# Convolution units summed into one half of a PSUM bank, with the convolution reading the bank

## The chip, the cores and the metric

The kernel runs on one core of one Trainium2 chip. The metric is the device time of one execution in microseconds (us), the median of several runs.

## What is computed

A trunk of two layers over 256 tokens of width 1024, in float32. Each layer is half a gated feed-forward block, a token mixer, cross-attention into 256 memory tokens, and half a feed-forward block, all with RMS norms. Layer 0's mixer is dilated window attention beside a gated linear recurrence (RG-LRU); layer 1's is a chunked gated DeltaNet with 8 heads of 128 and chunks of 64. What matters here are the two places with a causal convolution of four taps over time, right behind an input projection:

```
xc  = causal_dwconv(xr, conv_w) + conv_b                 # layer 0, 512 channels of h @ w_in
qkv = silu(causal_dwconv((h @ w_in)[..., :3*W], conv_w)) # layer 1, 3 x 1024 channels
q, k, v = split(qkv);  q, k = l2norm(q), l2norm(k)
kkt  = einsum(k*beta, k) * decay                         # per head and chunk of 64
sol  = triangular_solve(I + strict_lower(kkt), [v*beta, k*beta*exp(gcum)])
qk   = einsum(q, k) * decay                              # then the recurrence over four chunks
```

## The kernel before, in words

**Numbers.** Weights and activations are held as two fp32r parts, high (index 0) and low (1); a product is high x high + high x low + low x high. Activations lie with channels on partitions and 256 tokens along the row. A weight block of 1024 x 256 comes by DMA as two halves of four 128-row blocks (`raw`, L135); each is split by ScalarE (high part, L148) and then VectorE (low part, L149) into a `wt` tile of 128 x 1024 for each part. Four `wt` tiles exist, so two units' worth.

**Units.** A unit is 256 output columns of a projection, worked as two halves of 128 columns (j = 0, 1), each 8 k-steps. In `unit` each half takes a PSUM bank of its own, seen as 128 x 2 x 256: per k-step L190 multiplies the high weights with both parts of the activations (512 columns, both regions) and L194 the low weights with the high part (256 columns, region 0). When a half is summed up, `take` is called. `add` (L260, L261) brings the two regions together in SBUF: ScalarE copies region 1 to a tile `xn` (two buffers), VectorE adds region 0. `conv` then reads `xn`: ScalarE makes the last tap (L1022 in layer 1, with its own line in layer 0), VectorE adds the three others (L1025: rows of 255, 254 and 253 columns). Layer 0 has two such units (`lru_in`), layer 1 twelve: k, q and v, four each. z units (`unit_t`, L206 and L210, whose stationary side is the activations) have no convolution and use `add`. `parts` (L232) is the form used in cross-attention: three 256-column matmuls per k-step, all into one region. In the mixers the banks come from one pool of three (`psw`); two other pools of banks (`pss`, `psf`) hold small products.

**Layer 1 around the units.** After the softplus chain (small VectorE steps) the cumulative decay goes through a transpose (L1007) and `gt` (L1008) by DMA (`gd`, then four loads of `e`, L1067) to GpSimd, which adds a mask to each of four `e` tiles (L1071); ScalarE makes exps of them (L1076). GpSimd also makes the inverse roots `rs_dn` (L331) of the heads' square sums (L1054, `ss` at L1057), which VectorE uses in `hb_all` (L1098), `nb_all` (L1097) and `rq_all` (L1145). `na` (L1119) is the k x k product (L1113) times `e`. For a group of two head pairs `na` goes by DMA (L1123, L1178) into `nb`, where VectorE inverts 16x16 blocks in 15 pairs of steps (`tm` L1183, `ti` L1185), and by DMA again (L1191, L1197) into `tu`, with which TensorE builds the inverse of the whole triangle (L1218, L1226).

**Order.** Units are written in a fixed order (k0 k1 q0 q1 k2 v0 k3 v1 z0, then v3 z1 beside the first group's recurrence, v2 q2 q3 z2, and z3 beside the second's), with a few steps put off by a count of half units. The compiler's scheduler then sets the order of each engine's instructions; an engine executes them in that order, each waiting for its own inputs and for the buffers that it writes. Two engines do not touch one bank at the same time: an instruction waits until the other engine's instructions on that bank that stand ahead of it are done.

Of the kernel before, what the change touches and what calls it, by code (L numbers as in the profile page):

```python
# [18 lines left out]
P = 128  # L19
# [47 lines left out]
class Net:  # L67
# [166 lines left out]
    def unit_split(self, name, c0, mov, dst, tokens=False):  # L234

        wts = self.w(name, c0)
        bank = self.bank_w()
        for j, ks in STEADY:
            js = slice(j * P, j * P + P)
            for k in ks:  # L240
                w, m = wts[k // 4][:, k % 4], mov[:, k]
                a, b = (m, w) if tokens else (w, m)
                self.parts(bank[:, j], [a[:, i, js] for i in range(2)], [b[:, i] for i in range(2)], k == 0, k == KD - 1)
            if j and ks.stop == KD:
                self.split(dst, bank)
            yield

    def unit_t(self, name, c0, mov, take):

# [509 lines left out]
    def mixer0(self, mid, kT_mem, mem_mov, gnext):  # L759
# [4 lines left out]
        with tc.tile_pool(name="m0", bufs=1, reuse_waits="tile") as mp:  # L764
# [10 lines left out]
            self.covered([self.mem_key(c, mem_mov, kT_mem) for c in range(2)], mp, C_MIX)  # L775

            def lru_in(c):
                yield from self.unit("ab_w_in", 1536 + c * 256, mov, lambda j, ps: conv(2 * c + j, ps), lead=c == 0)

            def conv(f, ps):  # L780
                x = mp.tile([P, S], F32, name="xn", bufs=2)
                self.add(x, ps)
                tap = lambda i: self.col(C_LCW + 4 * i + f)
                xc[f] = mp.tile([P, S], F32, name="xc", bufs=4)
                nc.scalar.activation(xc[f], x, AF.Identity, scale=tap(3), bias=self.col(C_CONVB + f))
                for i in (2, 1, 0):
                    d = 3 - i
                    nc.vector.scalar_tensor_tensor(xc[f][:, d:], x[:, :S - d], tap(i), xc[f][:, d:],
                                                   op0=OP.mult, op1=OP.add)
# [162 lines left out]
    def mixer1(self, mid, kT_mem, mem_mov, gnext):  # L952
# [4 lines left out]
        with tc.tile_pool(name="m1", bufs=1, reuse_waits="tile") as mp:  # L957
# [56 lines left out]

                return mp.tile([P, 4, P], F32, name=name, bufs=bufs)

            def conv(y, j, f, ps):

                x = mp.tile([P, S], F32, name="xn", bufs=2)
                self.add(x, ps)  # L1020
                tap = lambda i: self.dcw[:, 24 * i + f:24 * i + f + 1]
                nc.scalar.activation(y[:, j], x, AF.Copy, scale=tap(3))  # L1022
                for i in (2, 1, 0):
# [277 lines left out]
            def unit(step):  # L1301
# [4 lines left out]
                if kind == "z":  # L1306
# [4 lines left out]
                    return  # L1311
                a = "qkv".index(kind)
                y = mp.tile([P, 2, S], F32, name="y", bufs=YB)
                yield from self.unit("dn_w_in", a * 1024 + c * 256, mov,
                                     lambda j, ps: conv(y, j, a * 8 + 2 * c + j, ps))
                twice = 2 if step in TWICE else 1
                silu(y, twice)
                if kind == "k":
# [96 lines left out]
```

## Time and profile before

| | us |
|---|---|
| median of 3 runs (least, greatest) | 1266.36 (1265.66, 1267.34) |
| profiled execution | 1266.04 |
| its span; around it | 1264.3; 1.7 |
| TensorE busy | 1244.4 |
| VectorE busy | 936.0 |
| ScalarE busy | 747.1 |
| GpSimd busy | 85.7 |

The profile is of one execution. Times in its rows count from the start of the span. An idle engine matters only where it ends a wait of the engine that sets the end; so the table says little by itself, and the waits by stretch, further down, say more. [...] Layer 0's mixer with its two units stands at about 213 to 227 us, layer 1's twelve units at about 795 to 921.

### The profile page before, as it was taken

Reading aid. Unit: us, or ns where it says so; the run is one execution under the profiler, and the core shown is the slowest. Engines: PE = TensorE matmul, PEld = TensorE weight load, DVE = VectorE, ACT = ScalarE, POOL = GpSimd, SP = SyncE. Lnnn points to the kernel's source line nnn. Section 1 sums busy time; section 2 is a strip of 40 time slices with the busy share of each in tenths; the row PEclk is TensorE's granted clock in tenths of the full one; section 3 lists DMA queues with packets and bytes.
Section 4 is the critical chain, followed back from the end, with each engine's and each line's share of the span. In section 5 each row is a group of like instructions: output and inputs, shape, how many; then the busy total and the mean of one; then the engine's idle time right before and its main releaser. Section 6 shows DMA issues by size and latency. Waiting matters only on the chain.

```text
span 1264.3 us, 20349 instructions
## 1 busy us (share of the span) xinstructions
PE 1244.4 (98%) x7726; PEld 1107.4 (88%) x7726; DVE 936.0 (74%) x1591; ACT 747.1 (59%) x1270; POOL 85.7 (7%) x101
## 2 busy tenths in 40 slices
PE   7999999999999999999999999999999999999998
PEld 6888889888998888888888888888899998888887
DVE  6887967787668778766877756999767768777753
ACT  5766545875555655545656544775747555665543
POOL 1000020000101000011000001130001101000000
PEclk9999999999999999999999999999999999999999
DMA  7766585543544565556556555656433644565551
GB/s 240 224 209 197 183 257 187 178 141 124 193 135 150 184 195 186 178 185 234 177 187 192 187 188 175 164 172 173 137 97 106 200 134 153 184 197 184 176 192 65
DMA packets 228409, 221.86 MB, mean 175 GB/s; under 512 B 14920, under 2 KB 226008, under 8 KB 228184
## 3 DMA queue, kind: packets, MB, share of 16 engines
q1 hardware_dynamic: 227384, 217.42, 54.9%
q0 software_dynamic: 928, 3.15, 0.9%
q8 instruction: 60, 0.98, 0.3%
q14 instruction: 37, 0.30, 0.1%
HBM read 215.03 MB, written 5.51 MB: 174 GB/s over the span
## 4 chain that ended last, share of the span: by engine, by line
PE 76%; issue 17%; DVE 2%; DMA 2%; POOL 1%; ACT 1%; SPq 0%; POOLq 0%; DVEq 0%
PE psw L190 16%; PE pss L190 13%; PE psw L194 8%; PE psf L190 8%; PE pss L194 7%; PE psw L232 6%; PE psf L194 4%; PE psf L232 3%; PE pss L232 2%; PE psw L206 1%; PE pss L1218 1%; PE psf L1226 1%; PE psw L210 1%; DVE y L1025 1%; PE pss L1226 1%
## 5 line engine op out<-in xcount | busy, mean ns | idle before, releaser
L149 DVE TENSOR_TENSOR wt<-raw,wt 128x1024 fp32r<-128x1024 f32 (+1 forms) x406 | 484.8, 1198 | 204.9 <-ACT wt L148 202.9
L148 ACT ACTIVATE wt<-raw 128x1024 fp32r<-128x1024 f32 (+1 forms) x406 | 418.1, 1036 | 174.4 <-PE psw L194 58.0
L190 PE MATMUL psw<-x,wt 128*128 128x512 f32 x856 | 308.7, 397 | 3.2 <-DVE xn L261 3.0
L194 PE MATMUL psw<-x,wt 128*128 128x256 f32 x856 | 223.6, 282 | 0.0
L190 PE MATMUL pss<-x,wt 128*128 128x512 f32 x536 | 195.4, 396 | 1.0 <-ACT wt L148 1.0
L190 PEld LDWEIGHTS psw<-x,wt 128*128 128x128 f32 x856 | 159.2, 188 | 31.3 <-DVE xn L261 3.6
L194 PEld LDWEIGHTS psw<-x,wt 128*128 128x128 f32 x856 | 161.1, 188 | 8.8 <-issue 0.2
L194 PE MATMUL pss<-x,wt 128*128 128x256 f32 x536 | 140.3, 282 | 0.5 <-DVE wt L149 0.5
L190 PE MATMUL psf<-x,wt 128*128 128x512 f32 x344 | 124.1, 393 | 0.0
L190 PEld LDWEIGHTS pss<-x,wt 128*128 128x128 f32 x536 | 101.4, 189 | 18.8 <-ACT wt L148 1.4
L194 PEld LDWEIGHTS pss<-x,wt 128*128 128x128 f32 x536 | 101.6, 190 | 6.5 <-DVE wt L149 1.0
L194 PE MATMUL psf<-x,wt 128*128 128x256 f32 x344 | 89.5, 281 | 0.0
L326 POOL TENSOR_TENSOR acc<-acc,sq 128x256 f32<-128x256 f32 x49 | 44.5, 909 | 662.1 <-ACT sq L324 661.8
L190 PE MATMUL pss<-h,wt 128*128 128x512 f32 x242 | 87.0, 397 | 0.0
L190 PE MATMUL psw<-h,wt 128*128 128x512 f32 x242 | 86.9, 396 | 0.0
L190 PEld LDWEIGHTS psf<-x,wt 128*128 128x128 f32 x344 | 64.6, 188 | 11.0
L194 PEld LDWEIGHTS psf<-x,wt 128*128 128x128 f32 x344 | 64.8, 188 | 3.8
L194 PE MATMUL pss<-h,wt 128*128 128x256 f32 x242 | 66.0, 280 | 0.0
L194 PE MATMUL psw<-h,wt 128*128 128x256 f32 x242 | 66.0, 280 | 0.0
L190 PE MATMUL psf<-h,wt 128*128 128x512 f32 x176 | 63.3, 397 | 0.0
L190 PEld LDWEIGHTS pss<-h,wt 128*128 128x128 f32 x242 | 45.5, 188 | 9.9
L190 PEld LDWEIGHTS psw<-h,wt 128*128 128x128 f32 x242 | 45.4, 188 | 9.9
(379 smaller groups left out, 2130.2 us busy)
## 6 DMA issues: line engine op xcount, KB each, us to landing
raw<-in_ffn_w_in_dram SPq DMA_DIRECT2D x176, 512.0 KB, 3.9
raw<-in_ffn_w_out_dram SPq DMA_DIRECT2D x80, 512.0 KB, 3.5
raw<-in_xa_wkv_dram SPq DMA_DIRECT2D x32, 512.0 KB, 3.7
raw<-in_dn_w_in_dram SPq DMA_DIRECT2D x32, 512.0 KB, 4.2
raw<-in_ab_w_in_dram SPq DMA_DIRECT2D x20, 512.0 KB, 3.9
raw<-in_xa_wq_dram SPq DMA_DIRECT2D x16, 512.0 KB, 3.3
raw<-in_xa_wo_dram SPq DMA_DIRECT2D x16, 512.0 KB, 3.4
raw<-in_ffn_w_out_dram SPq DMA_DIRECT2D x16, 256.0 KB, 2.6
```

The source lines that it names most:

```text
L148: nc.scalar.activation(a, r, AF.Copy)
L149: nc.vector.tensor_sub(b, r, a.bitcast(F32))
L190: nc.tensor.matmul(out.rearrange("p a s -> p (a s)"), w[:, 0, cols], mov[:, k].rearrange("p a s -> p (a s)"), start=k == start, stop=k == ...
L194: nc.tensor.matmul(out[:, 0], w[:, 1, cols], mov[:, k, 0], start=False, stop=False)
L206: nc.tensor.matmul(out.rearrange("p a s -> p (a s)"), mov[:, k, 0, tok], w.rearrange("p a s -> p (a s)"), start=k == 0, stop=k == KD - 1)
L210: nc.tensor.matmul(out[:, 0], mov[:, k, 1, tok], w[:, 0], start=False, stop=False)
L232: self.nc.tensor.matmul(out, a[u], b[w], start=first and i == 0, stop=last and i == 2)
L326: (eng or nc.gpsimd).tensor_add(self.acc, self.acc, sq)
L1025: nc.vector.scalar_tensor_tensor(y[:, j, d:], x[:, :S - d], tap(i), y[:, j, d:], op0=OP.mult, op1=OP.add)
L1218: nc.tensor.matmul(py[:, i], na[:, i], tu[:, 0, i], start=True, stop=True)
L1226: nc.tensor.matmul(pp[:, i], l[:, i], r[:, i], start=True, stop=True)
```

## The change

`unit_sum` takes the place of `unit` for the fourteen units that end in a convolution. It works with `parts`: three 256-column matmuls per k-step, all into one 128 x 256 region. The two halves of a unit use the two regions of one bank (the first unit of layer 0, whose halves are worked in turn, takes a bank for each). `conv` takes that region instead of a summed tile: ScalarE's tap and VectorE's three taps read PSUM. `add` and `xn` are gone from these units; z units and the gates' projection keep `add`.

```diff
+    def unit_sum(self, name, c0, mov, take, lead=False):
+
+        wts = self.w(name, c0)
+        bank = self.bank_w()
+        sums = [bank[:, 0], self.bank_w()[:, 0] if lead else bank[:, 1]]
+        for j, ks in (LEAD if lead else STEADY):
+            js = slice(j * P, j * P + P)
+            for k in ks:
+                w = wts[k // 4][:, k % 4]
+                self.parts(sums[j], [w[:, i, js] for i in range(2)], [mov[:, k, i] for i in range(2)], k == 0, k == KD - 1)
+            if ks.stop == KD:
+                take(j, sums[j])
+            if len(ks) == 4 or j:
+                yield
...
-                yield from self.unit("ab_w_in", 1536 + c * 256, mov, lambda j, ps: conv(2 * c + j, ps), lead=c == 0)
+                yield from self.unit_sum("ab_w_in", 1536 + c * 256, mov, lambda j, x: conv(2 * c + j, x), lead=c == 0)
...
-            def conv(y, j, f, ps):
+            def conv(y, j, f, x):
 
-                x = mp.tile([P, S], F32, name="xn", bufs=2)
-                self.add(x, ps)
                 tap = lambda i: self.dcw[:, 24 * i + f:24 * i + f + 1]
                 nc.scalar.activation(y[:, j], x, AF.Copy, scale=tap(3))
...
-                yield from self.unit("dn_w_in", a * 1024 + c * 256, mov,
-                                     lambda j, ps: conv(y, j, a * 8 + 2 * c + j, ps))
+                yield from self.unit_sum("dn_w_in", a * 1024 + c * 256, mov,
+                                         lambda j, x: conv(y, j, a * 8 + 2 * c + j, x))
```

`conv` of layer 0 loses the same two lines. Lines of the changed kernel are 15 higher from `add` on in the front part, 13 higher between the two mixers' `conv`s and 11 higher behind the second, so L148, L149 and L232 stay, L1025 becomes L1036, L1054 L1065, L1076 L1087, L1119 L1130 and L1218 L1229. There are 672 matmuls in these units where there were 448, each with its weight load.

The order moves too. Because the second half of a unit must wait for the convolution of the first, the scheduler puts another unit's half between them: k0's first, k1's first, k0's second, k1's second, and so on through the mixer.

TensorE before, at the end of k2's second half (`psw_8353`) and the start of v0 (`psw_8388`, a bank of its own for each half):

```order
L190 MATMUL psw_8353<-x2_79,wt_8223 128x512
L194 MATMUL psw_8353<-x2_79,wt_8223 128x256 x2
L190 MATMUL psw_8353<-x2_79,wt_8223 128x512
L190 MATMUL psw_8388<-x2_79,wt_8312 128x512 [waits DVE_49]
L194 MATMUL psw_8388<-x2_79,wt_8312 128x256
L190 MATMUL psw_8388<-x2_79,wt_8312 128x512
L194 MATMUL psw_8388<-x2_79,wt_8312 128x256
```

TensorE now, inside v0's first half (`psw_8452`, weights `wt_8371` and `wt_8395`), with k2's second half (`psw_8358`) in it; L1158 is the product of q0 and k0, L1065 are square sums of a head pair:

```order
L1158 MATMUL psf_8480<-y_8139,y_7941 128x128 [waits DVE_49]
L1158 MATMUL psf_8480<-y_8139,y_7941 128x128 x3
L232 MATMUL psw_8452<-x2_79,wt_8395 128x256 [waits Activation_49]
L232 MATMUL psw_8452<-x2_79,wt_8395 128x256
L1065 MATMUL pss_8577<-ones_86,th_8398 128x1 [waits PE_49,Activation_49]
L1065 MATMUL pss_8577<-ones_86,th_8398 128x1 x3
L232 MATMUL psw_8452<-x2_79,wt_8395 128x256 [waits DVE_49]
L232 MATMUL psw_8452<-x2_79,wt_8395 128x256 x3
L232 MATMUL psw_8358<-x2_79,wt_8255 128x256 [waits DVE_49]
L232 MATMUL psw_8358<-x2_79,wt_8255 128x256 x11
L232 MATMUL psw_8358<-x2_79,wt_8274 128x256 x12
L232 MATMUL psw_8452<-x2_79,wt_8395 128x256 x6
```

v0 now starts ahead of k2's second half and is cut in two by it; its weights `wt_8395` are waited for there, on ScalarE and then on VectorE.

ScalarE before, at the exps of the fourth `e` tile (`e_7919`); `wt_8397` and `wt_8434` are the weights of k3, the unit behind v0:

```order
L1076 ACTIVATE e_7919<-e_7919,ngc_7908 128x128 [waits Pool_49]
L1031 ACTIVATE th_8295<-y_8191 128x512 [waits DVE_49,Activation_49]
L1076 ACTIVATE e_7919<-e_7919,ngc_7908 128x128 x3
L260 ACTIVATE xn_8328<-psw_8303 128x256 [waits PE_49]
L260 ACTIVATE xn_8370<-psw_8353 128x256 [waits PE_49]
L148 ACTIVATE wt_8397<-raw_8194 128x4x256 [waits DMAHW6_49]
L1022 ACTIVATE y_8298<-xn_8328,dcw_91 128x256 [waits DVE_49]
L1048 ACTIVATE th_8338<-y_8191 128x512 [waits PE_49]
L1141 ACTIVATE q1_8340<-y_8191 128x256
L1022 ACTIVATE y_8298<-xn_8370,dcw_91 128x256 [waits DVE_49]
L148 ACTIVATE wt_8434<-raw_8299 128x4x256 [waits DMAHW7_49]
```

ScalarE now, at the same exps (`e_7938`); `wt_8395` is the second half of v0's weights, `wt_8465` the first of k3's:

```order
L1087 ACTIVATE e_7940<-e_7940,ngc_7927 128x128 x3
L1042 ACTIVATE th_8350<-y_8237 128x512 [waits DVE_49,Activation_49]
L1087 ACTIVATE e_7938<-e_7938,ngc_7927 128x128 [waits Pool_49]
L1087 ACTIVATE e_7938<-e_7938,ngc_7927 128x128 x3
L1033 ACTIVATE y_8353<-psw_8358,dcw_91 128x256 [waits PE_49]
L148 ACTIVATE wt_8395<-raw_8238 128x4x256 [waits DMAHW5_49]
L1059 ACTIVATE th_8398<-y_8237 128x512 [waits DVE_49]
L1152 ACTIVATE q1_8400<-y_8237 128x256
L148 ACTIVATE wt_8465<-raw_8240 128x4x256 [waits DMAHW6_49,PE_49]
```

Behind the exps stood the weights of k3, and now there are still those of v0's second k-half, which TensorE wants ahead of k2's second half. On GpSimd the first `rs_dn` of the burst, which stood between the first and the second `e`, now stands behind the fourth.

TensorE before, at the first use of the inverse (L1218 with `tu_8381`); `psw_8941` is z1, and v3 (both halves) stands ahead of it:

```order
L206 MATMUL psw_8941<-wt_8853,x2_79 128x512 [waits DVE_49]
L210 MATMUL psw_8941<-wt_8853,x2_79 128x256
L206 MATMUL psw_8941<-wt_8853,x2_79 128x512
L210 MATMUL psw_8941<-wt_8853,x2_79 128x256
L1218 MATMUL pss_8759<-tu_8381,na_8290 128x128 [waits DMAHW1_49]
L1218 MATMUL pss_8759<-tu_8381,na_8290 128x128 x3
L206 MATMUL psw_8941<-wt_8853,x2_79 128x512
```

TensorE now, at the same place (L1229); `psw_8869` is v3's first half, `psw_9041` is z1:

```order
L232 MATMUL psw_8869<-x2_79,wt_8785 128x256 [waits DVE_49]
L232 MATMUL psw_8869<-x2_79,wt_8785 128x256 x11
L1124 MATMUL psf_8885<-y_8554 128x128 x4
L232 MATMUL psw_8869<-x2_79,wt_8800 128x256 x12
L1229 MATMUL pss_8850<-tu_8445,na_8345 128x128 [waits DMAHW1_49]
L1229 MATMUL pss_8850<-tu_8445,na_8345 128x128 x3
L206 MATMUL psw_9041<-wt_8882,x2_79 128x512 [waits DVE_49]
L210 MATMUL psw_9041<-wt_8882,x2_79 128x256
```

v3's second half and the first 12 matmuls of z1 stood ahead of the first use of the inverse and stand behind it now.

## Rows read from the trace of the kernel before

**Rows 1.** The page, busy time of the engines and their share of the span.
```profile
PE 1244.4 (98%) x7726; PEld 1107.4 (88%) x7726; DVE 936.0 (74%) x1591; ACT 747.1 (59%) x1270; POOL 85.7 (7%) x101
```

**Rows 2.** Waits of TensorE, 700 to 960 us: who for whom, total, times, longest.
```profile
PE psw L190 <- DVE xn L261: 3.0, 2, 1.5
PE pss L1294 <- DVE qk L1285: 1.6, 2, 1.3
```

**Rows 3.** Busy time by stretch: stretch, length, engines (instructions), clock, DMA share, GB/s.
```profile
213.00:229.00 16.00, 15.82 (x91) 13.65 (x90) 15.53 (x29) 10.86 (x20) 0.00 (x0) 1.00 0.55 174
815.00:830.00 15.00, 13.54 (x92) 12.14 (x90) 12.92 (x28) 9.71 (x27) 10.31 (x11) 1.00 0.55 170
842.00:861.00 19.00, 18.68 (x123) 16.72 (x122) 18.02 (x65) 14.69 (x34) 3.08 (x2) 1.00 0.50 148
```

**Rows 4.** Timeline of TensorE: start, duration, line, operation, tiles, forms, count.
```profile
201.01 4.36 PE L232 MATMUL psw<-m,wt 128*128 128x256 f32 x36
...
602.13 0.39 PE L190 MATMUL pss<-x,wt 128*128 128x512 f32 x1
...
603.18 0.39 PE L190 MATMUL pss<-x,wt 128*128 128x512 f32 x1
```

**Rows 5.** Groups of VectorE by form, 785 to 925: count, busy, mean ns, idle before.
```profile
L149 DVE TENSOR_TENSOR wt<-raw,wt 128x1024 fp32r<-128x1024 f32 x33 | 40.1, 1217 | 2.7 <-ACT wt L148 2.6
...
L1025 DVE SCALAR_TENSOR_TENSOR y<-xn,dcw,y 128x254 f32<-128x254 f32 x24 | 11.3, 476 | 0.1
L261 DVE TENSOR_TENSOR xn<-psw,xn 128x256 f32<-128x256 f32 x25 | 10.3, 416 | 0.5 <-ACT xn L260 0.4
...
L301 DVE TENSOR_TENSOR x<-xn,x 128x256 fp32r<-128x256 f32 x8 | 3.0, 417 | 0.0
```

**Rows 6.** Groups of ScalarE by form, 785 to 925.
```profile
L148 ACT ACTIVATE wt<-raw 128x1024 fp32r<-128x1024 f32 x34 | 35.8, 1059 | 7.1 <-PE psw L194 6.3 <-PE psw L210 0.8
L1022 ACT ACTIVATE y<-xn,dcw 128x256 f32<-128x256 f32 x24 | 11.9, 505 | 5.5 <-DVE xn L261 5.5
L260 ACT ACTIVATE xn<-psw 128x256 f32<-128x256 f32 x25 | 9.3, 377 | 4.8 <-PE psw L190 4.1 <-DVE y L1025 0.7
```

**Rows 7.** Timeline of VectorE at the decays, the burst and the inversion's start.
```profile
815.11 0.28 DVE L1008 COPY gt<-pss 16x128 f32<-16x128 f32 x1
...
825.10 1.26 DVE L1098 TENSOR_TENSOR hb_all<-ss,rs_dn 128x4 f32<-128x4 f32 x1 [1.01 <-POOL rs_dn L331]
826.28 1.56 DVE L1025 SCALAR_TENSOR_TENSOR y<-xn,dcw,y 128x253 f32<-128x253 f32 x1
...
834.47 0.86 DVE L1119 SCALAR_TENSOR_TENSOR na<-psf,nb_all,e 128x128 f32<-128x128 f32 x3
...
841.85 0.18 DVE L1183 TENSOR_TENSOR tm<-nb,ti 64x15 f32<-64x15 f32 x1
```

**Rows 8.** Timeline of GpSimd at the burst.
```profile
822.52 1.56 POOL L1071 TENSOR_TENSOR e<-e,dn_negup 128x512 f32<-128x512 f32 x1 [2.37 <-DMA e<-gd]
824.04 1.03 POOL L331 TENSOR_TENSOR rs_dn<-ss,mhalf 128x4 f32<-128x4 f32 x1
825.05 3.94 POOL L1071 TENSOR_TENSOR e<-e,dn_negup 128x512 f32<-128x512 f32 x3
```

**Rows 9.** Timeline of TensorE at v0's halves and the first use of the inverse.
```profile
828.24 0.50 PE L190 MATMUL psw<-x,wt 128*128 128x512 f32 x1 [1.46 <-DVE xn L261]
...
829.74 0.95 PE L1054 MATMUL pss<-ones,th 128*128 128x1 f32 x8
...
834.61 0.50 PE L190 MATMUL psw<-x,wt 128*128 128x512 f32 x1 [1.52 <-DVE xn L261]
...
869.98 1.16 PE L1218 MATMUL pss<-tu,na 128*128 128x128 f32 x8 [0.51 <-DMA tu<-d]
```

**Rows 10.** Chain of waits around the first inversion's end: start, us, what.
```profile
861.37 4.12 DMA d<-ti
...
865.55 4.38 DMA tu<-d
```

More of the change, by code (lines that the diff above doesn't have):

```diff
@@ L777, in lru_in, with conv @@
             def lru_in(c):
-                yield from self.unit("ab_w_in", 1536 + c * 256, mov, lambda j, ps: conv(2 * c + j, ps), lead=c == 0)
-            def conv(f, ps):
-                x = mp.tile([P, S], F32, name="xn", bufs=2)
-                self.add(x, ps)
+                yield from self.unit_sum("ab_w_in", 1536 + c * 256, mov, lambda j, x: conv(2 * c + j, x), lead=c == 0)
+            def conv(f, x):
                 tap = lambda i: self.col(C_LCW + 4 * i + f)
@@ L1015, in four @@
                 return mp.tile([P, 4, P], F32, name=name, bufs=bufs)
-            def conv(y, j, f, ps):
-                x = mp.tile([P, S], F32, name="xn", bufs=2)
-                self.add(x, ps)
+            def conv(y, j, f, x):
                 tap = lambda i: self.dcw[:, 24 * i + f:24 * i + f + 1]
```

## The prediction

> **What bounds the kernel now.** The page comes first: TensorE is busy 98% of the span [rows 1], so the change is worth what it does to TensorE's few waits and what it adds to TensorE's work, and freed VectorE or ScalarE time counts only where one of these engines ends a wait. The list of TensorE's waits in the second mixer then gives what there is to win: 3.0 us in two waits for the add that frees a bank, and 1.6 us in two waits for the tile `qk` [rows 2]. The busy time by stretch shows why a small change of order matters there: VectorE is busy 18.02 of 19 us while the 16x16 blocks are inverted (842 to 861), and in 815 to 830 it is busy 12.92 of 15, with GpSimd busy too. In the first mixer, where two of the units lie, TensorE is busy 15.82 of 16 us and VectorE 15.53 [rows 3]. Last, the chain of waits: the inversion's last step, two DMAs (4.12 and 4.38 us) and then L1218, which starts at 869.98 after TensorE was idle for 0.5 us [rows 9, 10]. So at 869.98 two chains meet almost exactly: TensorE's own work, and the inversion through VectorE. Whatever the change does to the order around this point decides.
>
> **Matmuls.** 224 k-steps (28 halves of 8) go from one 512-column and one 256-column matmul to three of 256 columns. Three of the old steps take 603.18 - 602.13 = 1.05 us, 0.350 each. 36 matmuls of L232 take 4.36 us: 0.121 each, or 0.117 without the last one's tail (0.28) [rows 4]. Three are 0.350 to 0.363; I take 0.354, near the lower end, as the run is longer without a wait in it than a single unit. The sum is 224 x 0.004 = 0.9 us, between 0 and 2.9. All of it lies on TensorE's path. 224 more weight loads run beside the matmuls, as in the L232 rows.
>
> **Adds.** 28 times ScalarE's copy (0.38) and VectorE's add (0.42) go [rows 5, 6]. Consecutive VectorE instructions overlap by 0.08 (825.10 + 1.26 = 826.36, the next starts at 826.28 [rows 7]), so an add is 0.34 of a full queue: 9.5 us in all, of which 16 adds, 5.4 us, lie between the projection of the gates and the end of the first inversion. The three conv steps and the first product now read the bank. An add with one operand in the bank takes 416 ns and one with both in SBUF 417 [rows 5], so I cost the other source at nothing on VectorE; on ScalarE the bank's copy is 0.13 shorter (377 against 505 [rows 6]), off the path. [...]
>
> **The bank is shared.** A unit's second half cannot start before ScalarE and three VectorE steps have read the first: unloaded 0.51 + 3 x 0.40 = 1.7 us with the ends of the waits. The new order puts another unit's half between (k0, k1, k0, k1), 8 x 0.354 = 2.8 us. That leaves 1.1 us, less than one weight split (1.14 on VectorE, 1.06 on ScalarE). It also holds all four weight buffers during a pair: the splits for the next pair can start only when a pair's second halves have used their weights.
>
> **Where it binds: the burst on GpSimd.** I walk the new order with the durations of the rows. gt, which starts the decay chain, stands behind six halves instead of seven; less about 0.6 us of waiting for VectorE's steps ahead of it I put it at 812.9 instead of 815.11. The first `e` on GpSimd starts 7.4 us after gt [rows 7, 8], at 820.3; four of them (1.5 + 3.9) and then rs_dn, which in the new order stands behind all four instead of behind the first, end at 826.8. VectorE waits for that rs_dn at hb_all, as it did at 825.10 for one `e` and one rs_dn. Behind it on VectorE are q1's conv steps, four `na` and q1's silu step, to about 830; behind those on ScalarE the last four exps, k2's conv and the split of the second half of v0's weights (order of ScalarE), to 831.8, and VectorE's half of it to 833.0. TensorE gets there earlier. In the trace it was through k2 at 828.24 - 1.6 = 826.6 [rows 9]; in the new order k2's second half (2.8) is not yet done, 12 matmuls of v0 (1.4), sums and products (1.9, two groups like 829.74's) and, as an estimate, 1.9 us of waits and longer matmuls are (0.3 to 0.5 at each of four small products that stand behind silu or softplus steps on VectorE, 0.3 of matmuls): 829.0. So it waits 2.8 us, does the sums (0.9) and the four matmuls that stand before k2's second half, and starts that at 833.8. With v0's first half done at 837.3, and 0.6 and 0.7 us of waits after it (weights of k3, conv of v0), it ends all of v0 and k3's first half at 844.3; before, with its two waits of 1.5 us, the same work ends at 834.61 + 16 steps of 0.35 + sums of 0.95 = 841.2. **TensorE is 3.1 us later.** Bounds: -2.7 if nothing waits (the two old waits gone, 0.3 of matmuls), and +6 if a split misses at each of three further pairs by 1 us.
>
> **The inversion.** Its chain is as long as before from the last `na` (834.47 + 0.86 = 835.3, with 6.5 us of DMAs to 841.85 [rows 7]). In the walk the last `na` ends at 831.5, so the inversion starts at 838.0. Between its first and last step the new order has 18 conv steps for 16, 6 splits for 4 and no add for 5: +0.8 + 2.3 - 1.7, less 0.3 of small ones, +1.1 us on 861.3 - 841.85 = 19.5. It ends at 858.6, with half a microsecond of waits 859.2: **2.1 us earlier**, so L1218's inputs come at 867.9. Bounds: 0 if the idle grows as fast as the start moves, and 5.4 if all freed VectorE time counts.
>
> **What stands ahead of L1218.** In the new order v3's second half and 12 matmuls of z1 come behind the first L1218 instead of ahead: 14 k-steps, 4.95 us (order of TensorE). TensorE's own arrival is 869.98 - 0.5 - 4.95 + 3.1 + 0.1 = 867.7; the inputs come at 867.9. What is left to do from there is 4.95 longer, plus 0.2 of slower matmuls (7 halves). So the gain or loss is 867.9 + 4.95 + 0.2 - 869.98 = +3.1 us, with mixer 0 (4 halves, 0.1; its lead unit keeps two banks, and the one shared bank has 18 other matmuls, 3.2 us, in between) +3.2. The `qk` waits behind it [rows 2] keep their matmuls around them and stay. The profiled execution is 1266.04 (span 1264.3 and 1.7 around it), the median of the runs 0.3 more: 1266.04 + 3.2 + 0.3 = **1269.5**. Note that both limits stand near +3: to win, both the inversion and TensorE must come out better.
>
> **Rivals.** *Faster: the bank wait goes and nothing takes its place.* It decides at v0's weights: if they are split before TensorE wants them, at 829, TensorE arrives 3.0 us earlier less 0.9 of matmuls, and if the inversion then ends 7 us earlier, the time is 1266.4 - 2.1 = 1264.3, or 1262.7 if the `qk` waits go with it. For it speaks that a conv step with both tensors in SBUF took 1.56 beside GpSimd's `e`, when it is 0.48 otherwise [rows 5, 7], and a step that reads the bank would not be held if the bank operand frees it. [...] Against it: adds (5.4) and one hold (1.1) sum to 6.5 of the 7 needed, and hb_all itself now waits longer. 0.18.
>
> *Same: the pairing costs what the bank waits cost.* TensorE waits about 3.0 at the burst as before, the inversion ends 4.3 us earlier, and the extra matmuls remain: 1266.4 + 0.9 = 1267.3. For it: VectorE has 5.4 us less to do. 0.30.
>
> *Slower, as walked:* 1269.5, 0.40.
>
> *Much slower: the weight bursts.* With four buffers held by a pair, each of ScalarE's 1.06 and VectorE's 1.14 stands behind whatever conv steps are queued; missing by 1 us at some 4 more of the pairs between 800 and 920, with VectorE at 18.02 of 19 us [rows 3], gives +7, 1273.5. Against it: outside the burst VectorE gets 10% lighter. 0.12.
>
> **How the numbers follow.** A measurement can tell about 0.2%, 2.5 us, from no change. Faster by more is the first rival, 0.18; within it the second, 0.30; slower by more the last two, 0.52. The forecast is the likeliest case, 1269.5. The range runs from the better part of the first rival, 1263, to the bursts, 1274, and leaves about 1 in 10 on either side; the forecast's own range is 1268 to 1271.5.
>
> **What would show it.** Right: TensorE's waits name conv steps (L1036 in the new numbering) and the split at L148 or L149 near 829 to 834, 2 to 4 us; hb_all near 826 waits over 1 us for rs_dn; L1229 starts at 867 to 869 with a wait for the DMA of tu. Wrong: no wait of TensorE over 1 us between 820 and 845, or L1229 before 865 (then faster), or waits of half a microsecond spread over every pair (then the bursts); a k-step of three matmuls above 0.36 would mis-size the first term, and conv steps above 0.5 us the second.

## The result, and the profile after

The changed kernel takes 1275.19 us (median of 6 runs, 1274.23 to 1275.87) against 1266.28 for the kernel before on the same chip: a ratio of 1.0067, interval 1.0057 to 1.0077. It is slower by 8.9 us, where the forecast was slower by 3.2 and the range ended at 1274.0. The direction was right and the size was not. The profiled execution of the changed kernel took 1275.87, its span 1274.1.

The page's first part, which answers to [rows 1]: busy time, share and instructions of each engine.

```profile
PE 1250.7 (98%) x7950; PEld 1122.7 (88%) x7950; DVE 927.1 (73%) x1563; ACT 739.2 (58%) x1242; POOL 86.9 (7%) x101
```

VectorE's busy time fell by 8.9 us and ScalarE's by 7.9, with 28 instructions less on each. TensorE's busy time rose by 6.3. So the work that was to go has gone, and it shows nowhere in the time.

**Where the time came.** The matmul on `rcol` starts a mixer and the first matmul of L190 on `m` follows it; these rows of TensorE's timeline bound layer 1's mixer (after; before they stand at 784.35 and 943.75).

```profile
22.61 0.38 PE L379 MATMUL pss<-ident,rcol 128*128 128x128 f32 x2
...
786.89 0.43 PE L379 MATMUL pss<-ident,rcol 128*128 128x128 f32 x2 [0.21 <-POOL rcol L346]
...
953.59 0.48 PE L190 MATMUL psw<-m,wt 128*128 128x512 f32 x1
```

Layer 1's mixer takes 166.70 us, 7.3 more than its 159.40 before. From the first `rcol` matmul (20.75 before) to the second are 764.28 us against 763.60: layer 0's part costs 0.7. In single profiles this varies (762.97 to 763.79 in the kernels whose layer 0 has `unit`, mm256 apart, 763.13 to 764.76 in those with `unit_sum`), and the two means are 0.7 apart too. The remaining 1.9 us of the two spans' 9.8 lie ahead of the first `rcol` matmul, in the start-up, which the change doesn't touch and which stands at 20.75 to 22.61 in the kernels of this study. Below, "the mixer's stretch" is this 159.4 or 166.7; it repeats within about half a microsecond between kernels with the same code in it, and the median of a kernel says the rest.

TensorE's waits, 700 to 970 us, after (who for whom, total, times, longest); they answer to [rows 2].

```profile
PE psf L1158 <- DVE na L1130: 2.4, 1, 2.4
PE pss L1305 <- DVE qk L1296: 2.1, 2, 1.3
PE psw L232 <- ACT wt L148: 1.5, 1, 1.5
PE pss L1229 <- DMA tu<-d: 0.6, 1, 0.6
PE psw L232 <- DVE wt L149: 0.6, 2, 0.4
PE psw L232 <- DVE ti L1196: 0.5, 1, 0.5
```

The two waits for the bank add, 3.0 us in all, are gone. In their place stand 2.4 for the chain through `na`, 1.5 for v0's weights, and 1.1 for the next weights and for the inversion's steps that the conv steps are queued among. That is +2.0; `qk` adds 0.5 and `tu` 0.1: about 2.6 us of the mixer's 7.3 are waits of TensorE.

The burst on GpSimd, after (timeline; it answers to [rows 8]), and VectorE's steps ([rows 7]).

```profile
821.66 2.23 POOL L1082 TENSOR_TENSOR e<-e,dn_negup 128x512 f32<-128x512 f32 x1 [1.38 <-DMA e<-gd]
824.56 4.50 POOL L1082 TENSOR_TENSOR e<-e,dn_negup 128x512 f32<-128x512 f32 x3 [0.67 <-DMA e<-gd]
829.03 1.03 POOL L346 TENSOR_TENSOR rs_dn<-ss,mhalf 128x4 f32<-128x4 f32 x1
```

```profile
815.27 0.27 DVE L1021 COPY gt<-pss 16x128 f32<-16x128 f32 x1
...
823.13 1.84 DVE L149 TENSOR_TENSOR wt<-raw,wt 128x1024 fp32r<-128x1024 f32 x1
...
830.10 0.16 DVE L1109 TENSOR_TENSOR hb_all<-ss,rs_dn 128x4 f32<-128x4 f32 x1 [3.33 <-POOL rs_dn L346]
...
842.41 1.23 DVE L149 TENSOR_TENSOR wt<-raw,wt 128x1024 fp32r<-128x1024 f32 x1 [2.75 <-ACT wt L148]
...
843.95 0.17 DVE L1194 TENSOR_TENSOR tm<-nb,ti 64x15 f32<-64x15 f32 x1
```

`rs_dn` now stands behind all four `e` and ends at 830.06; VectorE has waited 3.33 us for it with everything else queued behind `hb_all`. Then TensorE, after ([rows 9]):

```profile
832.59 1.16 PE L1158 MATMUL psf<-y 128*128 128x128 f32 x8 [2.38 <-DVE na L1130]
835.27 0.79 PE L232 MATMUL psw<-x,wt 128*128 128x256 f32 x2 [1.52 <-ACT wt L148]
...
874.15 1.16 PE L1229 MATMUL pss<-tu,na 128*128 128x128 f32 x8 [0.64 <-DMA tu<-d]
```

And TensorE's granted clock behind these two waits, after (stretch, length, engines, clock, DMA share, GB/s).

```profile
832.00:835.00 3.00, 1.16 (x8) 0.97 (x8) 2.71 (x10) 2.89 (x7) 0.00 (x0) 0.93 0.29 87
835.00:838.00 3.00, 2.73 (x12) 2.71 (x13) 2.62 (x6) 1.04 (x3) 0.90 (x1) 0.50 0.44 103
838.00:841.00 3.00, 3.00 (x16) 3.00 (x15) 0.40 (x3) 0.00 (x0) 1.12 (x2) 0.50 0.76 186
841.00:844.00 3.00, 3.00 (x24) 2.85 (x23) 1.59 (x3) 2.21 (x3) 0.00 (x0) 0.93 0.00 0
```

From shortly before 835 to about 841.5 TensorE runs at 0.50 of the full clock; in the profile of the kernel before, the same stretches are at 1.00:

```profile
835.00:838.00 3.00, 3.00 (x19) 2.66 (x18) 3.00 (x8) 3.00 (x6) 0.00 (x0) 1.00 0.29 89
838.00:841.00 3.00, 3.00 (x23) 2.70 (x22) 3.00 (x6) 2.23 (x4) 0.00 (x0) 1.00 0.88 198
```

In after TensorE is busy from 835.27 on and gets less done: 16 matmuls in 838 to 841, 24 in the next 3 us. What it costs is read from the chain that ended last (start, us, what):

```profile
836.06 1.60 PE pss L1065 x8
837.66 3.64 PE psw L232 x16
...
841.32 1.07 ACT wt L148
...
842.41 1.23 DVE wt L149
...
844.03 0.08 DVE tm L1194
...
849.73 1.41 PE psw L232 x12
...
853.44 0.79 PE pss L1065 x8
...
861.19 1.55 PE psw L232 x12
...
862.77 1.07 ACT wt L148
...
863.86 1.23 DVE wt L149
865.09 0.07 DVE tm L1194
...
865.67 4.30 DMA d<-ti
```

The eight products of L1065 take 1.60 there and 0.79 later in the same chain; 16 matmuls take 3.64, and at 1.41 for 12 they would take 1.88; the two ahead of them took 0.79, and the same two behind the same wait take 0.50 at the full clock (fill14, below). That is 0.81 + 1.76 + 0.29, **2.9 us**. TensorE's busy time in the mixer bears this out (stretch, length, engines, clock, DMA share, GB/s: before, after, and two kernels of the experiments that have the matmuls of after and the clock at 1.00, own_bank and nomask_after).

```profile
784.35:943.75 159.40, 154.01 (x1042) 139.09 (x1042) 133.01 (x330) 107.37 (x234) 18.44 (x18) 1.00 0.54 150
786.89:953.59 166.70, 158.65 (x1234) 151.68 (x1234) 125.04 (x306) 100.53 (x210) 19.69 (x18) 0.98 0.51 143
786.38:945.31 158.93, 154.05 (x1233) 148.18 (x1234) 122.86 (x306) 100.43 (x210) 16.95 (x18) 1.00 0.54 151
786.02:946.71 160.69, 155.72 (x1233) 148.83 (x1234) 124.40 (x306) 98.70 (x210) 11.90 (x14) 1.00 0.53 149
```

Of the 7.3 us, 2.7 are idle time of TensorE (166.70 - 158.65 against 159.40 - 154.01) and 4.6 are busy time. After's busy time is 2.9 above nomask_after's, which is what the chain gives for the half clock. The other 1.7, by which nomask_after is above own_bank, come in kernels with the two halves in one bank; no row sorts them out. The longer row of matmuls adds nothing here: own_bank is at 154.05 and the kernel before at 154.01.

The chain also shows that this time is not TensorE's alone: ScalarE's split of the next weights (841.32) waited 5.28 us until these matmuls had released the buffer, VectorE's half of the split (842.41) is queued ahead of `tm` (844.03), and `tm` is the first step of the inversion. The same happens at the inversion's end (862.77 to 865.09): the last `tm` stands behind a split that waited for 12 matmuls. So the half clock puts back both chains that meet at L1229, the inversion and TensorE's own, and neither hides the other.

### The profile page after: what moved, and what is told of

Its sections match the earlier page's. It is cut to its first block, busy times and chain, and to the rows that moved or that the text cites. A ratio compares the mean times of both kernels' runs of the same rounds, so it can differ in the third digit from the quotient of the medians.

```text
span 1274.1 us, 20744 instructions
## 1 busy us (share of the span) xinstructions
PE 1250.7 (98%) x7950; PEld 1122.7 (88%) x7950; DVE 927.1 (73%) x1563; ACT 739.2 (58%) x1242; POOL 86.9 (7%) x101
## 4 chain that ended last, share of the span: by engine, by line
PE 78%; issue 15%; DVE 2%; DMA 2%; ACT 1%; POOL 1%; SPq 0%; POOLq 0%; DVEq 0%; ACTq 0%
PE psw L190 15%; PE pss L190 13%; PE psw L232 9%; PE psf L190 8%; PE psw L194 8%; PE pss L194 7%; PE psf L194 4%; PE psf L232 3%; PE pss L232 2%; PE psw L206 2%; PE pss L1229 1%; PE psf L1237 1%; PE psw L210 1%; DVE wt L149 1%; PE pss L1237 1%
## 5 line engine op out<-in xcount | busy, mean ns | idle before, releaser
L149 DVE TENSOR_TENSOR wt<-raw,wt 128x1024 fp32r<-128x1024 f32 (+1 forms) x406 | 485.6, 1200 | 215.2 <-ACT wt L148 213.1
L148 ACT ACTIVATE wt<-raw 128x1024 fp32r<-128x1024 f32 (+1 forms) x406 | 418.0, 1036 | 186.9 <-PE psw L194 44.7
L190 PE MATMUL psw<-x,wt 128*128 128x512 f32 x624 | 226.4, 396 | 0.3 <-DVE xc L801 0.3
L190 PE MATMUL pss<-x,wt 128*128 128x512 f32 x536 | 195.8, 397 | 1.0 <-ACT wt L148 1.0
L194 PE MATMUL psw<-x,wt 128*128 128x256 f32 x624 | 162.7, 281 | 0.0
L190 PEld LDWEIGHTS psw<-x,wt 128*128 128x128 f32 x624 | 116.9, 188 | 20.9 <-issue 0.5
L190 PE MATMUL psf<-x,wt 128*128 128x512 f32 x352 | 128.0, 395 | 0.0
L232 PE MATMUL psw<-x,wt 128*128 128x256 f32 x960 | 123.6, 285 | 2.9 <-ACT wt L148 1.5
L194 PEld LDWEIGHTS psw<-x,wt 128*128 128x128 f32 x624 | 117.5, 188 | 6.7 <-issue 0.2
L232 PEld LDWEIGHTS psw<-x,wt 128*128 128x128 f32 x960 | 117.7, 191 | 4.5 <-ACT wt L148 1.7
L190 PEld LDWEIGHTS pss<-x,wt 128*128 128x128 f32 x536 | 101.6, 190 | 18.9 <-ACT wt L148 1.4
L341 POOL TENSOR_TENSOR acc<-acc,sq 128x256 f32<-128x256 f32 x49 | 44.5, 908 | 662.7 <-ACT sq L339 662.4
L190 PE MATMUL pss<-h,wt 128*128 128x512 f32 x242 | 87.0, 397 | 0.0
L190 PE MATMUL psw<-h,wt 128*128 128x512 f32 x242 | 86.9, 396 | 0.0
L190 PEld LDWEIGHTS psf<-x,wt 128*128 128x128 f32 x352 | 66.5, 189 | 11.4
L194 PEld LDWEIGHTS psf<-x,wt 128*128 128x128 f32 x352 | 66.7, 190 | 3.9
L190 PE MATMUL psf<-h,wt 128*128 128x512 f32 x176 | 63.3, 397 | 0.0
```

Source lines behind the costliest of these rows:

```text
L148: nc.scalar.activation(a, r, AF.Copy)
L149: nc.vector.tensor_sub(b, r, a.bitcast(F32))
L190: nc.tensor.matmul(out.rearrange("p a s -> p (a s)"), w[:, 0, cols], mov[:, k].rearrange("p a s -> p (a s)"), start=k == start, stop=k == ...
L194: nc.tensor.matmul(out[:, 0], w[:, 1, cols], mov[:, k, 0], start=False, stop=False)
L232: self.nc.tensor.matmul(out, a[u], b[w], start=first and i == 0, stop=last and i == 2)
L341: (eng or nc.gpsimd).tensor_add(self.acc, self.acc, sq)
```

## The experiments

The mixer's stretch is split at the first use of the inverse (L1218 before, L1229 after). All in us; the ratio is to the kernel before on the same chip.

| kernel | median | ratio, interval | stretch | to first use | behind it |
|---|---|---|---|---|---|
| before | 1266.3 to 1267.0 | 1 | 159.4 | 85.6 | 73.8 |
| after | 1275.19 | 1.0067, 1.0057 to 1.0077 | 166.7 | 87.3 | 79.4 |
| m1_only | 1274.84 | 1.0064, 1.0049 to 1.0079 | 166.7 | 87.3 | 79.4 |
| m0_only | 1268.12 | 1.0010, 1.0000 to 1.0019 | 159.3 | 85.5 | 73.8 |
| own_bank | 1267.06 | 1.0002, 0.9992 to 1.0012 | 158.9 | 84.8 | 74.2 |
| own_l1 | 1266.34 | 0.9996, 0.9987 to 1.0004 | 159.1 | 84.0 | 75.1 |
| mm256 | 1271.87 | 1.0044, 1.0029 to 1.0059 | 163.3 | 86.4 | 76.9 |
| copy | 1272.79 | 1.0044, 1.0030 to 1.0059 | 165.6 | 84.7 | 80.8 |
| own_copy | 1269.16 | 1.0019, 1.0010 to 1.0028 | 161.6 | 83.9 | 77.7 |
| fill14 | 1274.33 | 1.0061, 1.0046 to 1.0077 | 165.7 | 86.0 | 79.6 |
| nohb_after | 1271.05 | 1.0032, 1.0020 to 1.0044 | 163.4 | 84.1 | 79.4 |
| nohb_before | 1267.27 | 1.0001, 0.9991 to 1.0010 | 159.8 | 86.2 | 73.7 |
| nomask_after | 1269.19 | 1.0022, 1.0013 to 1.0032 | 160.7 | 80.0 | 80.7 |
| nomask_before | 1264.70 | 0.9984, 0.9975 to 0.9993 | 158.4 | 82.3 | 76.1 |

**One layer at a time.** m1_only and m0_only make the change in layer 1 or in layer 0 alone; the other layer's units and `conv` are as before. For m1_only, in layer 0:

```diff
-                yield from self.unit_sum("ab_w_in", 1536 + c * 256, mov, lambda j, x: conv(2 * c + j, x), lead=c == 0)
+                yield from self.unit("ab_w_in", 1536 + c * 256, mov, lambda j, ps: conv(2 * c + j, ps), lead=c == 0)
```

> The change in layer 1's mixer alone (12 units); layer 0's two units as before. Theory A (the loss is the chain gt, e, rs_dn, hb_all, conv steps, exps, weight split that holds TensorE once near 832 to 835, and a stretch at half clock behind it): nearly all of it stays, 1273 to 1275 us, with the same two waits of 2.4 and 1.5 us and 5 to 6 us at a granted clock of 0.5. Theory B (every unit pays: longer k-steps, four reads of the bank): 12/14 of the loss, 1273.9, but with waits spread over all units. The two differ in where the time goes, not in the sum.

> The change in layer 0's mixer alone (2 units). Theory A: 0.1 of matmuls and about 0.5 of a wait, 1266.5 to 1267.2. Theory B: 2/14 of 8.9, 1267.6. If it is 1268 or more, the loss is partly from the start of the kernel (a shift of the first feed-forward block), which neither theory has.

m1_only is 8.1 us slower than before and shows the same waits, and 0.51 and 0.63 of the clock in 832 to 836 and 836 to 840. m0_only is 1.3 slower by its median (its interval ends at no difference) and 0.9 by its rows up to layer 1's mixer. So the loss is layer 1's, and layer 0's term is small, though not the 0.1 of the forecast; 1268.12 is more than either theory had. A wait of 0.3 us for `xc` (TensorE, L190 <- L801) stands in both kernels that change layer 0 and not before.

**Is it the shared bank?** own_bank gives each half a bank of its own; three matmuls per k-step, no add, and the convolution reading PSUM all stay.

```diff
-        bank = self.bank_w()
-        sums = [bank[:, 0], self.bank_w()[:, 0] if lead else bank[:, 1]]
+        sums = [None, None]
...
+            if sums[j] is None:
+                sums[j] = self.bank_w()[:, 0]
```

> As the changed kernel, but each half of a unit takes a bank of its own; the conv still reads PSUM four times and there are still three matmuls per k-step. Both halves of a unit then follow each other again and weights come free one unit at a time. Theory A: the burst's chain holds other work or nothing; the time is 1265 to 1269, and TensorE's clock stays at 1.0 if no wait is longer than about 2 us. Theory B: the loss stays, 1273 to 1275, since the matmuls and the reads are the same.

TensorE's waits of own_bank, 700 to 970, and its clock:

```profile
PE pss L1306 <- DVE qk L1297: 2.1, 2, 1.3
PE pss L1230 <- DMA tu<-d: 1.2, 1, 1.2
PE psw L232 <- DVE y L1037: 1.2, 1, 1.2
```

```profile
832.00:836.00 4.00, 2.45 (x20) 2.17 (x19) 3.65 (x11) 4.00 (x10) 0.00 (x0) 1.00 0.20 63
836.00:840.00 4.00, 4.00 (x38) 4.00 (x36) 3.45 (x7) 3.55 (x5) 1.03 (x1) 1.00 0.46 85
```

The time is that of the kernel before, and layer 1's mixer is half a microsecond shorter. All that the change loses in layer 1 comes with the shared bank: with the order of halves and of GpSimd's steps that follows from it, since own_bank keeps the matmuls, the missing adds and the reads of PSUM, while the two halves of a unit follow each other there as before the change. own_bank's own order is another one as well (its `rs_dn` stands ahead of the four `e`, at 820.45), so it doesn't tell which part of that order costs what. It tells one thing more: 28 adds less on VectorE and on ScalarE, and two waits of 1.5 us for them gone, bring nothing that can be measured here. Waits of 1.2 for `y` and 1.2 for `tu` took their place.

own_l1, own banks in layer 1 alone with layer 0 as before, was to take away layer 0's loss.

> Layer 1's units with a bank for each half, summed in one region and read there by the conv; layer 0's two units as in the kernel before. Theory A: layer 0 gives back what the change cost there (0 to 1.3 us by the kernel with layer 0 alone), so 1265.5 to 1266.8, the same as the kernel before or 0.1% better. Theory B has no term that would let it be below 1267.

1266.34 against 1266.97 of before in the same batch: not to be told from the kernel before, nor by the intervals from own_bank. It has the lowest median of the versions with the convolution in PSUM, and is no gain.

**The matmuls alone.** mm256 is the kernel before with three 256-column matmuls per k-step and nothing else changed.

```diff
-            self.mm3(banks[j], wts, slice(j * P, j * P + P), mov, ks)
+            for k in ks:
+                w = wts[k // 4][:, k % 4]
+                for i, (u, m) in enumerate(((0, 0), (0, 1), (1, 0))):
+                    nc.tensor.matmul(banks[j][:, m], w[:, u, js], mov[:, k, m], ...
```

> The kernel before with its k-step as three 256-column matmuls into the same two regions (region 0 twice, region 1 once) and the add kept: the price of the 224 matmuls alone. Theory A: +0.9 us (0 to 2.9), 1266.3 to 1269. Theory B: +3 or more.

The edit stands in `unit`, which all plain units call, and so it reached 2048 k-steps (9774 matmuls for 7726), not the 224 that the expectation counted. It is 5.1 us slower, 2.5 ns a k-step (1.8 to 3.6). This price is probably too high, as the clock of its profiled execution fell in layer 1's mixer (0.51 in 838 to 840). For the change's 224 k-steps it makes 0.6 us (0.4 to 0.8), within the forecast's bounds of 0 to 2.9 and a little under its 0.9; the busy times of own_bank and before, above, make it nothing.

**PSUM or SBUF as the source.** copy and own_copy put one copy of the region to SBUF by ScalarE ahead of the convolution, with the shared bank and with own banks.

```diff
-            def conv(y, j, f, x):
+            def conv(y, j, f, ps):
+                x = mp.tile([P, S], F32, name="xn", bufs=2)
+                nc.scalar.activation(x, ps, AF.Copy)
```

> The changed kernel, but ScalarE copies the summed region to a tile in SBUF and the conv reads that: the two halves still share a bank, which now comes free after one ScalarE copy (0.38 us) instead of after four reads through two queues. The scheduler then cuts halves into smaller pieces in between. Theory A: the reads no longer hang on VectorE's queue, so the wait at v0's weights is smaller (0 to 2 us) and the clock stays: 1266 to 1270. Rival (four buffers of weights held by a pair cost the time): 1272 or more.

> A bank for each half, summed in one region, copied to SBUF by ScalarE, conv from SBUF: the plain order of units, no add on VectorE, banks free after one copy. Theory A: the one wait of 1.2 us for conv steps that the kernel with its own banks showed goes, ScalarE has 28 copies of 0.38 us more than there: 1265 to 1267, about as before.

VectorE's conv steps of one width by form, 785 to 925, in after (count, busy, mean ns, idle before).

```profile
L1036 DVE SCALAR_TENSOR_TENSOR y<-psw,dcw,y 128x254 f32<-128x254 f32 x22 | 10.5, 477 | 0.2
```

From PSUM a step takes 477 ns, as from SBUF before ([rows 5], 476). In copy, with the source in SBUF, the mean of the same row is 518. It comes from a few held steps beside GpSimd's `e`, as in copy's timeline of VectorE:

```profile
818.93 1.48 DVE L1040 SCALAR_TENSOR_TENSOR y<-xn,dcw,y 128x254 f32<-128x254 f32 x1
821.53 2.94 DVE L1040 SCALAR_TENSOR_TENSOR y<-xn,dcw,y 128x253 f32<-128x253 f32 x2
```

Three steps of copy take about 1.5 us, three of own_copy 0.97 to 1.51, one of before 1.56 [rows 7]; none of the 72 of after or of the 72 of own_bank takes over 0.49. Few of these ran beside an `e`, but over all kernels the rows are plain: of the 12 conv steps from SBUF that did, ten took 0.97 to 1.56 (the two others had begun before the `e`); of the 11 from PSUM (one in after, two in own_bank, four in nohb_after) all took 0.45 to 0.48. The split of weights, with both operands in SBUF, is held too (1.84 at 823.13 in after, 1.23 elsewhere). So the steps that read the bank were not held here, as the forecast's first rival had it, but the copies don't gain or lose by it alone: copy is 2.4 us faster than after, own_copy 2.1 slower than own_bank, both with other orders and other waits (copy 1.8 for weights and 1.2 for `th`, own_copy 1.7 for weights) and with a fall of the clock in own_copy that own_bank's profile doesn't have. With the shared bank the stretch is 4.0 longer than with own banks here too. Both medians lie above what theory A expected (1266 to 1270 and 1265 to 1267), and copy's is what its rival named.

**The chain through rs_dn.** nohb_after and nohb_before take `hb` from the reciprocal that VectorE has at hand, not from GpSimd's `rs_dn`; the factor from the inverse root is left out of `hb`. Then nothing on VectorE waits for GpSimd's four `e`.

```diff
-                    nc.vector.tensor_mul(hb, ss, r)
+                    nc.vector.tensor_mul(hb, ss, r2)
```

> The changed kernel, with hb (the factor of v's rows) made from the reciprocal that VectorE has already, instead of from GpSimd's rs_dn: that leaves out the inverse root in hb, and takes away the one wait of VectorE for the rs_dn that stands behind GpSimd's four e. The order of TensorE stays but for a few rows. Theory A (that wait heads the chain to q1's conv steps, the exps and the weight split): the waits of 2.4 and 1.5 us fall to at most 1 us together, TensorE stays at a granted clock of 1.0, and the time falls by 5 to 7 us, to 1268 to 1270. Rival (the pairing starves TensorE of weights wherever it stands, the burst only shows it): the waits move to the next pair and the time falls by 2 us at most.

> The same edit in the kernel before (the inverse root in hb left out), as the control: TensorE's order is the same row for row. Theory A: VectorE's wait of 1.0 and the held 1.2 at hb go, the two waits of 1.5 us for a bank shrink to 1 to 2 us together, 1264.5 to 1266.

TensorE's waits at the burst and at the first use, nohb_after (timeline):

```profile
830.99 0.50 PE L232 MATMUL psw<-x,wt 128*128 128x256 f32 x2 [1.28 <-ACT wt L148]
...
869.49 1.16 PE L1229 MATMUL pss<-tu,na 128*128 128x128 f32 x8 [1.35 <-DMA tu<-d]
```

The wait of 2.4 for `na` is gone, the inversion starts 53.35 us into the mixer and not 57.06, and the kernel is 4.1 us faster than after. The control hardly moves. Both miss what was expected: a fall by 5 to 7 us with the clock at 1.00, and 1264.5 to 1266 for the control. So that chain is worth some 4 of the 7.3 us, and part of the half clock is in it: in nohb_after the clock is at 0.63 and 0.52 in 832 to 834 and 834 to 836 and at 1.00 behind, half as long as in after. Of the rest the two right columns of the table tell: against its control nohb_after reaches the first use 2.1 us earlier and needs 5.7 more behind it. TensorE now waits 1.35 for the inverse, because 14 k-steps that stood ahead of L1229 stand behind it.

**The burst without GpSimd.** nomask_after and nomask_before leave GpSimd's mask additions out and take the exponential with scale 0.

```diff
-                    nc.gpsimd.tensor_add(e, e, neg_up[:, None, :].to_broadcast([P, 4, P]))
+                    pass
...
-                            nc.scalar.activation(..., AF.Exp, bias=ngc[:, c, 2 * p + j:2 * p + j + 1])
+                            nc.scalar.activation(..., AF.Exp, scale=0.0)
```

> The changed kernel, and in mixer 1's softmax GpSimd's mask additions are left out and the exponential is taken with scale 0, so that every e is 1 (the mask and the scores don't enter the output). The burst that ran from gt through GpSimd's e additions to rs_dn and hb_all has lost its GpSimd part. Theory A (the wait of 2.4 us for the convolution, the weight wait of 1.5 us and the half clock behind them all come from that late chain): its time less that of nomask_before is at most +1.5 us: 0.6 for the matmuls, 0.7 for layer 0, and a little; no wait for na over 0.5 us, clock 1.00 from 820 to 850. Rival (the pairing of halves itself costs, whatever is in the burst): +4 us or more, with a long wait for na or wt still there.

> The kernel before with the same left out; the control for nomask_after. By both theories within 3 us of the kernel before: there the chain through e was beside 36 k-steps of TensorE and ended no wait over 0.5 us; what may move is the order, since the planner knows that the additions are gone.

TensorE's waits over half a microsecond, nomask_after:

```profile
PE pss L1304 <- DVE qk L1295: 2.1, 2, 1.2
PE psw L232 <- DVE wt L149: 1.0, 2, 0.8
PE pss L1228 <- DMA tu<-d: 0.9, 1, 0.9
```

The difference of the two is 4.5 us by the medians, and neither expectation holds whole. The long waits are gone and the clock is 1.00 from 820 to 852, as the theory of the late chain has it; but its 1.5 us are too few. By the profiles the pair differs by 2.3 in layer 1's mixer, 0.7 up to it and 0.3 in the start-up, 3.2 in all. The other 1.3 come from the two executions that were profiled: nomask_before's had a fall of the clock (below) and is 1.1 above its median, nomask_after's is 0.3 below its own. So with a burst that has no GpSimd part the mixer's loss falls from 7.3 to between 2.3 and 3.6, and that much remains with the pairing: `tu` 0.9 for none, `qk` 0.5, waits for weights, and the 1.7 us of TensorE's busy time above own_bank's.

**Is it the long wait that slows the clock?** fill14 is after with 14 matmuls of 256 columns, which nobody reads, ahead of L1158, so that TensorE works where it waited 2.4 us.

```diff
+                    pf = self.bank("s")
+                    for i in range(14 if p == 0 else 0):
+                        nc.tensor.matmul(pf[:, 0], mov[:, i % KD, 0, :P], mov[:, i % KD, 0], ...
```

> The changed kernel with 14 matmuls more of 256 columns, 1.6 us of TensorE's time, whose output is never read, between q0's square sums and the product of q0 and k0, where TensorE waited 2.4 us; the order around them stays. Theory A2 (the stretch at a granted clock of 0.5 comes from that wait, and costs 3 us by itself): the wait falls to 0.8, the half clock shrinks or goes, and the kernel with more work is faster, 1272 to 1273.5. Rival (the clock has another cause, or the second wait of 1.5 alone brings it): the stretch at 0.5 stays as long and the time is 1275 or more.

fill14's TensorE at the place, and its clock:

```profile
830.45 1.16 PE L1163 MATMUL psf<-y 128*128 128x128 f32 x8 [0.59 <-DVE na L1130]
833.13 0.50 PE L232 MATMUL psw<-x,wt 128*128 128x256 f32 x2 [1.52 <-ACT wt L148]
...
842.41 1.43 PE L232 MATMUL psw<-x,wt 128*128 128x256 f32 x10 [0.42 <-DVE wt L149]
```

```profile
832.00:836.00 4.00, 2.85 (x20) 2.65 (x21) 3.42 (x8) 1.90 (x4) 1.01 (x1) 0.93 0.41 96
836.00:840.00 4.00, 4.00 (x25) 4.00 (x25) 1.63 (x4) 1.39 (x2) 1.01 (x1) 0.64 0.60 140
```

The wait for `na` fell to 0.6 and the clock fell all the same, behind the wait of 1.52 for the weights. So the wait of 2.4 is not needed for a fall; but the fall is half as long, and here the price can be read. Both kernels come to the two matmuls behind the weights at the same time, counted from the start of the mixer: 48.36 us (833.13 - 784.77) in fill14 and 48.38 in after. They do the same work behind it. fill14 starts the ten matmuls 57.64 in, after 58.85 (845.74 - 786.89); the first `tm` comes at 55.81 and 57.06, the first use of the inverse at 86.03 and 87.26. So about half of the half clock costs 1.2 us on both chains, which is in keeping with 2.9 for the whole. The kernel with more work is faster by 1.0 in the mixer and 0.9 by the medians, whose intervals overlap: the expectation had the sign, not the size.

Beside this stands the kernel before, with waits of 1.46 and 1.52 [rows 9] and the clock at 1.00 behind both. Nor is a fall only the change's: nohb_before has 0.57 in 836 to 840 behind one wait of 2.4, and nomask_before 0.72 in 840 to 844 behind one of 1.1. The limit of about 2 us in own_bank's expectation, the author's estimate between before's 1.52 and after's 2.38, doesn't hold. Nor does a kernel always do the same: the mean clock of all six executions of after is 0.995 or 0.996, but of own_copy's ten it is 0.999 in four, which took 1267.85 to 1268.81, and 0.996 or 0.997 in six, which took 1269.08 to 1271.95. Which waits bring a fall stays open.

## Why the prediction was right in direction and too small

**What held.** The matmuls (0.9 forecast, 0 to 0.6 measured) and the conv steps from PSUM (no charge: 477 for 476). The walk through the burst: counted from the start of the mixer, gt at 28.4 (812.9 - 784.35 = 28.55 in the forecast), TensorE's release by ScalarE's split of v0's second weights at 48.4 (835.27 - 786.89) against 47.5, and TensorE waiting for `na` and the weights, 2.4 + 1.5 us where the forecast had one wait of 2.8 (without the waits it would have been through the products of L1158 at 44.5, 832.59 - 2.38 + 1.16 - 786.89, and the forecast had it there at 44.65). `hb_all` waited 3.3 us for `rs_dn`, for the reason given: it stands behind all four `e`. The two waits behind, 0.37 and 0.46, were put at 0.6 and 0.7. The 14 k-steps behind L1229: 5.15 forecast for the part behind the first use, 5.7 measured, of which 0.5 is `qk`. The length of the inversion up to L1229: 29.9 forecast, 30.2 measured. Of the forecast's signs, the one of L1229 failed: it was to start at 867 to 869, and counted from the same start of the mixer it came at 871.6 (784.35 + 87.26).

**The step that failed: the matmuls behind the burst, and with them the inversion's start.** The walk puts all of v0 and k3's first half behind the burst at the full clock, 0.117 a matmul, and lets the inversion follow the last `na` by 6.5 us of DMAs, 53.65 us into the mixer. Its first `tm` came at 57.06, 3.4 later. Of this 1.0 is the burst itself: GpSimd began the four `e` 1.2 earlier than walked but took 7.4 us for them with a wait inside, not 5.4, `hb_all` came 0.8 late and the last `na` ended at 48.15 (834.70 + 0.34 - 786.89) instead of 47.15. By that and the DMAs `tm` would have stood at 54.65. The other 2.4 are a link that the forecast didn't have: ahead of `tm` on VectorE is the split at 842.41, which had waited 2.75 us for ScalarE, which had waited 5.28 us for TensorE to release the weight buffer, as ScalarE's timeline has it:

```profile
841.32 1.06 ACT L148 ACTIVATE wt<-raw 128x1024 fp32r<-128x1024 f32 x1 [5.28 <-PE psw L232]
```

The forecast counted this split in VectorE's busy time only. And the matmuls that release the buffer ran at half clock, 3.64 us for 16: with 2.9 us less the split would have ended at 840.7, ahead of the last `na`'s DMAs. So the missing term is the half clock, 2.9 us, and its way through the weight buffer to the inversion; fill14, with about half of it, has `tm` and L1229 each 1.2 us earlier. In nohb_after and nomask_after, where the burst ends earlier, the first `tm` stands at 53.35 and 53.66. An earlier start alone would not have been enough: by the chain the inversion's last steps stand behind the split at 863.86, which waited for TensorE again, and VectorE was idle for only 0.1 us just before it.

**The limits moved together.** The forecast's own note, that the inversion and TensorE both stand near +3, is what made the miss come through whole: TensorE's arrival at L1229 is 86.6 us into the mixer (874.15 - 0.64 - 786.89) against 83.35, 3.3 late: 0.9 from the later release at the burst, 2.9 from the half clock, less 0.5 by which the two waits behind were shorter. The inputs are 3.7 late. They came late together; the wait that was left there is 0.64.

**In sum,** for layer 1: 3.1 forecast; 3.4 for the late start of the inversion (TensorE's 3.3 runs beside it and is not counted again), 0.3 for its length, 0.5 for `qk`, which was said to stay and rose from 1.6 to 2.1; 7.3. Layer 0: 0.7 for 0.1. That makes 8.0 of the medians' 8.9; the remaining 0.9 is about the scatter of the start-up and isn't settled.

**The rivals.** The faster one asked that nothing take the wait's place; something did in every order tried, with own banks too. "Same" named 1267.3 for the pairing and own_bank, without the pairing, takes 1267.1; that the two figures agree is chance. The bursts' 1273.5 was nearest in size, but not by its mechanism: outside 830 to 848 no wait for weights of half a microsecond stands in the list.

## What to carry to other kernels

Two sums in one bank aren't two buffers: here the readers of the first had to be done before the second could start (v0's second half started at 847.64, after 0.46 us of waiting, when the last conv step of its first half had ended at 847.50), the order of everything near it changed, and that cost more than the copies that were saved. When a walk ends a wait on the engine that sets the time, ask what that engine's matmuls release, and follow it to the next chain; and price the matmuls behind a wait at both levels of the clock (here 0.117 and 0.23 us for 256 columns) before giving a range. Time freed on an engine that is busy 74% was worth nothing here, as each wait that ended on it had a second chain right behind.

## What the runs showed that was not expected

TensorE's granted clock fell to 0.50 in the middle of a busy kernel, for nearly 7 us, behind waits of 2.38 and 1.52 us that 1.16 us of matmuls part. Matmuls of 256 columns then took 0.23 us each (3.64 for 16) and not 0.117. In layer 1's mixer it fell, for some 3 to 7 us, in the profiled executions of 9 of the 14 kernels (after, m1_only, fill14, copy, own_copy, mm256, both of the nohb pair and nomask_before), behind waits of 1.1 to 2.4 us. It stayed at 1.00 in those of the others, behind the kernel before's waits of 1.46 and 1.52 and behind own_bank's 1.2.

A conv step on VectorE with one operand in PSUM was never held by GpSimd (11 steps ran beside an `e`, 0.48 us at most), while with both in SBUF ten of 12 took two to three times as long.
